# Branch B's output projection as two Strassen quads of seven products, with a new list schedule

## The chip, the cores and the metric

The kernel runs on one core of one Trainium2 chip. The metric is the device time of one execution in microseconds. The program holds one layer (512 positions, model width 1024, feed-forward width 2816), all in 32-bit floats.

## The reference

```python
def _mixer(x, mem, ...):
    h = _rmsnorm(x, norm_mix_g)
    p_a, p_b, q, p_g = jnp.split(h @ w_in, IN_SPLITS, axis=-1)
    gb, gc, v = jnp.split(p_a, 3, axis=-1)
    y_a = (gb * _causal_dwconv(gc * v, conv_a_w)) @ w_a_out
    u, ug = jnp.split(p_b, 2, axis=-1)
    u = _causal_dwconv(u * jax.nn.sigmoid(ug), conv_b_w) + conv_b_bias      # 31 taps
    y_b = jax.nn.silu(_layernorm(u, ln_b_g, ln_b_b)) @ w_b_out
    ...                                    # cross-attention into 256 memory tokens: o
    y_c = o @ w_att_out
    g = jax.nn.sigmoid((p_g + b_gate).reshape(bsz, seq, 3, D_MODEL))
    return (g[:, :, 0] * y_a + g[:, :, 1] * y_b + g[:, :, 2] * y_c) @ w_o

def reference(x, mem, ...):
    x = x + _mixer(x, mem, ...)
    h = _rmsnorm(x, norm_ffn_g)
    gt, up = jnp.split(_causal_dwconv(h @ w_up, conv_ffn_w), 2, axis=-1)
    return _rmsnorm(x + (jax.nn.silu(gt) * up) @ w_down, norm_final_g)
```

The change is in `y_b = ... @ w_b_out`, a product of 512 by 1024 by 1024.

## The kernel before

**Arithmetic.** Each 32-bit operand is split into a high part (a cast on ScalarE, the profile's ACT) and a low part (the rest, a subtraction on VectorE, DVE), and a product is three products of parts: high by high, low by high, high by low. Weights come in blocks of 512 KB (128 partitions by 1024). `split_job` turns a loaded block `wf` into `whi` (L494, ACT) and `wlo` (L498, DVE). In some places ACT writes the negated high part instead and an accumulating transfer, issued by GpSimd (POOL), adds the block once more, so that DVE is spared (`lo_from`, L515).

**Quads.** Most projections use Strassen's scheme in Winograd's form: two by two blocks of weights times two by two blocks of the activation in seven products instead of eight, f = 1 to 7 (`multiply`, L674). One such product is 24 matmuls of 256 columns here. Its operands are the blocks of the activation b00, b10, b11 and the sums t4 to t7, each with a high and a low part; `quad_loads` brings the weights and forms their sums in place (jobs s5, s6, s7, s3, by accumulating transfers where `by_dma` is set); `quad_reads` takes the results out of the banks of PSUM and adds them (r1 to r7). The three output projections of the branches were not quads: `merge_product` (L1406) runs eight plain units (four column groups m by two halves g), each 24 matmuls of 512 columns (L1416 to L1418), on `ybh`, `ybl` in branch B (br = 1). DVE multiplies the results by the gates (job weigh, L1449), and sums them over the branches into `mg` (L1467), whose four quarters are the operands of the last projection `w_o`. That one is a hand-written scheme of seven products a, b, f, c, d, e, g on `mgh` and `mgl`; the weights of a, b and d (`whoh`, `whol`) are split early and held in tiles that the quads' forms used before.

**Order.** TensorE's (PE) order is written out in `seq`, and hooks after certain products put the merge and other work in. All other instructions are jobs of the list scheduler `Jobs`: it runs when the program is built, gives each job a due time from the product that needs it, shifts it by the table `LATER`, holds back the kinds of job named in `AHEAD` until so long before their due time, and writes the instructions into each engine's queue in the order that comes out. So a change of a table, of a cost or of a job can move work of any engine in the whole program. Weights come in through six buffers `wf` and rings of tiles; four pairs of `whi` and `wlo` exist (`UNIT_BUFS`). SP issues plain loads, POOL accumulating ones; each issues in order.

**Stages.** In order of time: memory keys and values, the mixer's input projection with convolutions and attention between, the branches' output projections, `w_o` and the residual `x`, then `w_up` in quads with convolution and gate, `w_down`, the final norm and the output.

Of the kernel before, what the change touches and what calls it, by code (L numbers as in the profile page):

```python
# [8 lines left out]
F32 = mybir.dt.float32  # L9
F32R = mybir.dt.float32r  # L10
AF = mybir.ActivationFunctionType
ALU = mybir.AluOpType
# [49 lines left out]
PACE = 0.3  # L62
SEEN = {"PE": 0.2, "ACT": 0.14, "DVE": 0.12}
# [7 lines left out]
    "ACT high": -44, "ACT r1 glu": -9, "ACT r4 gate": 44, "ACT r4 up": -3, "ACT r5 glu": -7,  # L71
    "ACT sigmoid": 12, "ACT tap 1": 3, "ACT tp 3": -111, "ACT vh": 40, "ACT wh mix 5": 8,
# [9 lines left out]
    "ACT fh h2 t4": 5, "ACT high": 10, "ACT r5 glu": 10, "ACT r5 up": 5, "ACT sigmoid": 20,  # L82
    "ACT tap 1": 150, "ACT vh": 5, "ACT wh pd a": 5, "DVE rd g": 5, "DVE tot1": 10,
    "POOL s5 q": 10, "POOL wadd e": 5, "POOL xa": 40, "SP ld e 0": 20,
# [246 lines left out]
def hybrid_block_kernel(  # L331
# [139 lines left out]
    def split_job(unit, key, n_k, n, after, wide=None, lo_from=None, held=None):  # L471
# [62 lines left out]
    def block(w, col, k):  # L534

        return w[col // 256, k]
# [89 lines left out]
    def quad_loads(q, w, col0, col1, by_dma=False, take=("wf",), after=()):  # L626
# [9 lines left out]
        split_job((q, 1), u, 4, 256, [("ld", u)])  # L636
        split_job((q, 2), v, 4, 256, [("ld", v)])
# [22 lines left out]
        split_job((q, 4), r, 4, 256, [("ld", r)])  # L660
# [32 lines left out]
    def quad_reads(q, first, second, ring, after=()):  # L693
# [13 lines left out]
        def add(t, b):  # L707
# [13 lines left out]
            [(q, 3), ("r6", q)], use=[bank("b"), first])  # L721
        job(("r4", q), "ACT", actv(512), lambda: nc.scalar.activation(
# [327 lines left out]
    for h in range(HEADS):  # L1050
# [18 lines left out]
        for tp in range(2):  # L1069
# [23 lines left out]
            job(("exp", h, tp), "ACT", 0.84, exps,  # L1093
# [107 lines left out]
    for p in range(4):  # L1201
        job(("sg", p), "ACT", actv(1024), lambda p=p: nc.scalar.activation(
# [154 lines left out]
    for p in range(4):  # L1357
        split_pair(("acc", p), ("ybh", p), ("ybl", p), [("swish", p)])
# [25 lines left out]
    for p in range(4):  # L1384
# [13 lines left out]
    PARTS = {0: ("yah", "yal"), 1: ("ybh", "ybl"), 2: ("oh", "ol")}  # L1398
    PARTS_READY = {
        0: [("low", ("ya", p)) for p in range(4)],  # L1400
        1: [("low", ("acc", p)) for p in range(4)],
        2: [("ol", h, d) for h in range(HEADS) for d in range(2)],
    }
    W_OUT = {0: w_a_out, 1: w_b_out, 2: w_att_out}
# [26 lines left out]
    for br in (2, 0, 1):  # L1431
        for m in range(4):
            for g in range(2):
                unit_job(("merge", br, m, g), block(W_OUT[br], m * 256, g), lo_by_dma=br != 1 and 2 < 2 * m + g < 6)
# [9 lines left out]
            job(("sigmoid", br, m), "ACT", 2 * scaled_act(512), sigmoid,  # L1444
                ready_of(("gate", br, m // 2), m % 2) + [("ldp",)], use=[gate])
            for j in range(2):
# [12 lines left out]
            elif br == 1:  # L1459
                for r in range(2):  # L1460
                    part = ("mg", r, m // 2)

                    def merged(m=m, gate=gate, r=r, part=part):
# [9 lines left out]
                        weighed + [("sum", 0, m)] + ([("sum", 1, m - 1, r)] if m % 2 else []),  # L1473
# [5 lines left out]
    late_rows = [("merge", 1, 0, 1)]  # L1479
# [28 lines left out]
    }  # L1508

# [8 lines left out]
    for i in range(2):  # L1518
# [17 lines left out]
        for p, key, after in (  # L1536
# [5 lines left out]
            split_job(("wo", p, i), ("wo", key, i), 2, 512, [after], held=WO_HELD.get((p, i)))  # L1542
# [194 lines left out]
    for q in range(QUADS):  # L1737
# [12 lines left out]
        job(("silu", q), "ACT", actv(1024), lambda q=q: nc.scalar.activation(  # L1750
# [18 lines left out]
    for do in (  # L1769
# [41 lines left out]
        (GATE[1, 1], 3): lambda: [pe_merge(1, m) for m in range(4)],  # L1811
# [55 lines left out]
    first = [(UP[0], 1), (UP[0], 2), "tr2", (UP[1], 1), "tr3", (UP[1], 2), (UP[2], 1), (UP[0], 5), (UP[2], 2), (UP[0], 6), (UP[1], 5), (UP[0], 7), (UP[0], 3), (UP[0], 4), (UP[1], 6), (UP[2], 5), (UP[1], 7), (UP[2], 6), (UP[1], 4), (UP[1], 3)]  # L1867
# [254 lines left out]

    for p in DOWN:
# [13 lines left out]
    for t in range(NT):  # L2137
# [7 lines left out]
        else:  # L2145
# [11 lines left out]
        job(("sv", t), "DVE", 0.75, lambda t=t: left_scaled(t),  # L2157
            [("rc", t)] + ([("rd", "end", 1)] if t == 2 else []))
# [65 lines left out]
```

## Time and profile before

| what | value |
|---|---|
| time, median of 3 runs | 926.52 us (926.11 to 926.7) |
| profiled execution | 926.69 us, of which the span of the trace is 924.7 us |
| granted TensorE clock | 0.999 |
| busy: PE, DVE, ACT, POOL | 916.1, 838.7, 669.0, 127.0 us |
| moved by DMA | 190.60 MB |

The span runs from the first to the last instruction; 2.0 us of the profiled execution lie outside it. The engines run side by side, so their busy times overlap; an engine's idle time matters only where another waits for it.

### The profile page before, as it was taken

The page shows a single profiled execution, that of the slowest core. Times are in us where ns is not written, and L with a number is a line of the kernel's source. Part 1 is how long each engine was busy: PE and PEld are TensorE (multiplying, and loading weights), DVE is VectorE, ACT ScalarE, POOL GpSimd, SP SyncE. Part 2 cuts the span into 40 slices and gives each one's busy share as a digit, 9 for nine tenths or more (in the row PEclk, how much of TensorE's full clock was granted, in tenths as well). Part 3 has the DMA queues.
Part 4 walks back from the last instruction along what each step waited for, and adds up shares of the span by engine and source line. Part 5 has one row for each costly group of instructions (what it writes and reads, how often), then busy time and mean ns, then how long its engine had stood idle before and what let it go on. Part 6 is the DMA issues. An engine that isn't in the chain of part 4 may idle for free.

```text
span 924.7 us, 16795 instructions
## 1 busy us (share of the span) xinstructions
PE 916.1 (99%) x6677; PEld 861.9 (93%) x6677; DVE 838.7 (91%) x952; ACT 669.0 (72%) x911; POOL 127.0 (14%) x153
## 2 busy tenths in 40 slices
PE   9999999999999999999999999999999999999997
PEld 8999999999989999999899888899999999988886
DVE  6997999979989999999986788898989889999987
ACT  7567988859889877778855763767676676765566
POOL 0111121100111211110100001021211121002120
PEclk9999999999999999999999999999999999999999
DMA  9999877956678789887855598499999996789962
GB/s 353 369 297 225 177 133 142 233 134 114 180 190 223 159 189 226 187 197 202 198 119 168 164 318 181 117 219 302 283 222 233 218 182 120 201 269 319 260 131 91
DMA packets 54222, 190.60 MB, mean 206 GB/s; under 512 B 6144, under 2 KB 6272, under 8 KB 54144
## 3 DMA queue, kind: packets, MB, share of 16 engines
q0 software_dynamic: 20880, 75.24, 46.0%
q1 hardware_dynamic: 32976, 114.02, 34.3%
q8 instruction: 52, 0.85, 0.4%
q10 hardware_dynamic: 288, 0.27, 0.1%
q14 instruction: 26, 0.21, 0.1%
HBM read 185.31 MB, written 4.19 MB: 205 GB/s over the span
## 4 chain that ended last, share of the span: by engine, by line
PE 94%; DMA 3%; ACT 1%; DVE 0%; SPq 0%; issue 0%; POOLq 0%; DVEq 0%; ACTq 0%
PE bank L674 57%; PE bank L446 7%; PE bank L447 7%; PE bank L445 7%; PE bank L1416 5%; PE bank L1418 5%; PE bank L1417 5%; DMA wf<-in_w_up 2%; PE bank L928 2%; DMA wf<-in_w_v 1%; ACT whi L494 1%; PE ss L801 0%; PE bank L1165 0%; PE bank L1653 0%; DVE wlo L498 0%
## 5 line engine op out<-in xcount | busy, mean ns | idle before, releaser
L494 ACT CAST whi<-wf 128x1024 fp32r<-128x1024 f32 (+1 forms) x190 | 197.4, 1042 | 91.7 <-PE bank L674 47.1
L498 DVE TENSOR_TENSOR wlo<-wf,whi 128x1024 fp32r<-128x1024 f32 (+1 forms) x184 | 222.0, 1211 | 28.5 <-ACT whi L494 27.9
L1237 ACT ACTIVATE tp<-u,pk 128x510 f32<-128x510 f32 (+22 forms) x184 | 119.4, 705 | 5.1 <-DVE acc L1244 4.8
L1244 DVE TENSOR_TENSOR acc<-acc,tp 128x1020 f32<-128x1020 f32 (+22 forms) x92 | 109.2, 1188 | 5.8 <-ACT tp L1237 3.8
L632 POOL DMA_DIRECT2D wf<-in_w_in x45 | 39.0, 873 | 236.3 <-DVE wlo L498 175.4
L674 PE MATMUL bank<-ft6h,whi 128*128 128x256 f32 x232 | 64.4, 277 | 0.7 <-ACT gt L701 0.7
L674 PE MATMUL bank<-ft5l,whi 128*128 128x256 f32 x232 | 64.4, 278 | 0.0
L674 PE MATMUL bank<-fb10h,whi 128*128 128x256 f32 x232 | 64.4, 277 | 0.0
L674 PE MATMUL bank<-ft6h,wlo 128*128 128x256 f32 x232 | 64.3, 277 | 0.0
L674 PE MATMUL bank<-ft5h,wlo 128*128 128x256 f32 x232 | 64.3, 277 | 0.0
L674 PE MATMUL bank<-fb00h,whi 128*128 128x256 f32 x232 | 64.3, 277 | 0.0
L674 PE MATMUL bank<-ft7h,whi 128*128 128x256 f32 x232 | 64.3, 277 | 0.0
L674 PE MATMUL bank<-ft7l,whi 128*128 128x256 f32 x232 | 64.3, 277 | 0.0
L674 PE MATMUL bank<-ft7h,wlo 128*128 128x256 f32 x232 | 64.3, 277 | 0.0
L674 PE MATMUL bank<-fb11h,whi 128*128 128x256 f32 x232 | 64.3, 277 | 0.0
L674 PE MATMUL bank<-ft5h,whi 128*128 128x256 f32 x232 | 64.3, 277 | 0.0
L674 PE MATMUL bank<-ft6l,whi 128*128 128x256 f32 x232 | 64.3, 277 | 0.0
L674 PE MATMUL bank<-fb00l,whi 128*128 128x256 f32 x232 | 64.2, 277 | 0.0
L674 PE MATMUL bank<-fb00h,wlo 128*128 128x256 f32 x232 | 64.2, 277 | 0.0
L674 PE MATMUL bank<-fb10h,wlo 128*128 128x256 f32 x232 | 64.1, 276 | 0.0
L674 PE MATMUL bank<-fb10l,whi 128*128 128x256 f32 x232 | 64.1, 276 | 0.0
L674 PE MATMUL bank<-fb11l,whi 128*128 128x256 f32 x232 | 64.1, 276 | 0.0
(401 smaller groups left out, 3170.5 us busy)
## 6 DMA issues: line engine op xcount, KB each, us to landing
wf<-in_w_in SPq DMA_DIRECT2D x50, 512.0 KB, 5.0
wf<-in_w_in POOLq DMA_DIRECT2D x45, 512.0 KB, 5.9
wf<-in_w_up POOLq DMA_DIRECT2D x30, 512.0 KB, 7.6
wf<-in_w_up SPq DMA_DIRECT2D x29, 512.0 KB, 6.3
wf<-in_w_down SPq DMA_DIRECT2D x15, 512.0 KB, 4.6
wf<-in_w_att_out SPq DMA_DIRECT2D x8, 512.0 KB, 3.7
wf<-in_w_a_out SPq DMA_DIRECT2D x8, 512.0 KB, 4.2
wf<-in_w_b_out SPq DMA_DIRECT2D x8, 512.0 KB, 4.3
```

Of the source, the lines that this page charges most:

```text
L445: nc.tensor.matmul(ps, s_hi, w_hi, start=start, stop=False, skip_group_check=again)
L446: nc.tensor.matmul(ps, s_hi, w_lo, start=False, stop=False, skip_group_check=again)
L447: nc.tensor.matmul(ps, s_lo, w_hi, start=False, stop=stop, skip_group_check=again)
L494: nc.scalar.copy(parts[0], src())
L498: nc.vector.tensor_tensor(lo, src(), hi.bitcast(F32), op=ALU.subtract)
L632: nc.gpsimd.dma_start(out=tiles[key], in_=block(w, col[c], k), accum_op=ALU.add)
L674: nc.tensor.matmul(ps[:, c, :], w[:, k, at], a[k], start=first and n == 0, stop=i == 3 and n == 2, skip_group_check=again,)
L1237: nc.scalar.activation(two(("tp", p, s))[:, j, s:], two(("u", p))[:, j, : SEQ - s], AF.Copy, scale=weight(j),)
L1244: nc.vector.tensor_tensor(a, a, two(("tp", p, s))[:, :, s:], op=ALU.add)
L1416: nc.tensor.matmul(ps, w_hi[:, i, at], hi, start=first, stop=False)
L1417: nc.tensor.matmul(ps, w_hi[:, i, at], lo, start=False, stop=False)
L1418: nc.tensor.matmul(ps, w_lo[:, i, at], hi, start=False, stop=last)
```

## The change

Branch B's eight plain units become two quads, ("mq", 0) and ("mq", 1), run product by product in the order f = 1, 5, 2, 6, 7, 4, 3, the two in turn. The activation after its norm is formed as the seven operands, in halves: b00, b10, b11 are blocks of `acc`, t5, t7, t6, t4 are half sums on DVE, t7, t6 and t4 in place. The weights' sums s5, s6, s7, s3 are accumulating transfers. The results are read as in other quads, but the last one is weighed by the gate straight from its bank. The lows of `w_o`'s held weights for a and b now come by accumulating transfer (`WO_LOWS`) instead of from DVE, and the held tiles come free after the last quad's products. The rows of `x` for the residual are loaded after a product of the second quad. The scheduler's costs count 1.28 us for a load of ACT's function table at four jobs (`TABLE`); both tables are new, and the `w_up` stage starts with another order of products. The last output tile's left half is scaled and sent in two halves.

```diff
+TABLE = 1.28
...
 LATER = {
-    "ACT high": -44, "ACT r1 glu": -9, "ACT r4 gate": 44, "ACT r4 up": -3, "ACT r5 glu": -7,
...
+    "DVE h2 t4": -36, "DVE kl": -6, "DVE kt": 11, "DVE mgl a": 32, "DVE mgl f": 25,
...
 AHEAD = {
-    "ACT fh h2 t4": 5, "ACT high": 10, "ACT r5 glu": 10, "ACT r5 up": 5, "ACT sigmoid": 20,
+    "ACT kh": 40, "ACT r1 up": 80, "ACT r5 gate": 20, "ACT r5 up": 40, "ACT sg": 80,
...
             if held:
                 last = next(f for f in OPERAND if OPERAND[f] == held)
-                before = [(QUAD_ORDER[-1], last)]
+                before = [(("mq", 1), last)]
...
+        low = lambda f, c, k: block(w, col[c], k) if f in lows else None
+        split_job((q, 1), u, 4, 256, [("ld", u)], lo_from=low(1, 0, 0))
...
-    for p in range(4):
-        split_pair(("acc", p), ("ybh", p), ("ybl", p), [("swish", p)])
...
+    for e in range(2):
+        top, end = ("acc", e), ("acc", 2 + e)
+        done = lambda *ps: [("swish", p) for p in ps]
+        b00 = y_parts("b00", e, lambda e=e: rows_of(e, 0), done(e), [top])
+        b10 = y_parts("b10", e, lambda e=e: rows_of(2 + e, 0), done(2 + e), [end])
+        y_parts("b11", e, lambda e=e: rows_of(2 + e, 1), done(2 + e), [end])
...
+        job(("y", "t7", e), "DVE", dve(512), lambda e=e: nc.vector.tensor_tensor(
+            rows_of(e, 1), rows_of(2 + e, 1), rows_of(e, 1), op=ALU.subtract),
+            [Y5 + (e,)] + done(2 + e), use=[top, end])
...
-            for g in range(2):
-                unit_job(("merge", br, m, g), block(W_OUT[br], m * 256, g), lo_by_dma=br != 1 and 2 < 2 * m + g < 6)
+            for g in range(2) if br != 1 else ():
+                unit_job(("merge", br, m, g), block(W_OUT[br], m * 256, g),
+                         lo_by_dma=2 < 2 * m + g < 6)
...
+                quad = ("mq", m // 2)
+                if m % 2 == 0:
+                    quad_loads(quad, w_b_out, m * 256, m * 256 + 256, by_dma=True, lows=MQ_LOWS)
+                    quad_reads(quad, ("y", m), ("y", m + 1), ANY, all_but_4=True)
...
+                    def weigh_last(m=m, gate=gate, at=at, quad=quad):
+                        t = two(gate)[:, :, at]
+                        nc.vector.scalar_tensor_tensor(
+                            t, halves(("bank", quad, "a")), -1.0, t, op0=ALU.mult, op1=ALU.mult)
...
-    late_rows = [("merge", 1, 0, 1)]
+    late_rows = [(("mq", 1), 1)]
...
+    WO_LOWS = [(p, i) for p in "ab" for i in range(2)]
...
-        (GATE[1, 1], 3): lambda: [pe_merge(1, m) for m in range(4)],
+        (GATE[1, 1], 3): lambda: [
+            multiply_job(("mq", q), f, "y") for f in (1, 5, 2, 6, 7, 4, 3) for q in range(2)],
...
-    first = [(UP[0], 1), ..., (UP[2], 1), (UP[0], 5), (UP[2], 2), (UP[0], 6), (UP[1], 5), (UP[0], 7), ...]
+    first = [(UP[0], 1), ..., (UP[2], 1), (UP[0], 5), (UP[1], 5), (UP[0], 6), (UP[2], 2), (UP[0], 7), ...]
...
+        if t < last:
+            job(("sv", t), "DVE", 0.75, lambda t=t: left_scaled(t),
+                [("rc", t)] + ([("rd", "end", 1)] if t == 2 else []))
+        else:
+            for i in range(2):
+                job(("sv", t, i), "DVE", 0.4, lambda i=i: last_scaled(i), [("rc", t)])
```

The order moves at three places that the prediction speaks of. The first is DVE between the last sum of the merge and the third product of `w_o`, f. `mg` are the merged quarters, `mgl` the low parts of operands of `w_o`'s products, `bank` results. Before, f's sum is the first of the two 1024-wide rows on `mg_796_6183` and its low part `mgl_850_6468`:

```order
L1467 TENSOR_TENSOR mg_835_6393<-g_338_2496,g_746_5812 128x512
L1467 TENSOR_TENSOR mg_839_6400<-g_338_2496,g_746_5812 128x512
L1550 TENSOR_TENSOR mg_796_6183<-mg_839_6400,mg_796_6183 128x1024
L1572 TENSOR_TENSOR mgl_841_6408<-mg_835_6393,mgh_840_6406 128x512
L451 SCALAR_TENSOR_TENSOR mg_795_6181<-mg_796_6183,mg_795_6181 128x1024
L1572 TENSOR_TENSOR mgl_850_6468<-mg_796_6183,mgh_846_6449 128x1024
```

After, on the same engine, from the read of the second quad's last product (bank_794_6194) on; f's sum is `mg_845_6613` and its low part `mgl_865_6694`, c's are `mg_828_6480` and `mgl_864_6692`:

```order
L715 TENSOR_TENSOR y_790_6185<-y_790_6185,bank_794_6194 128x2x256
L1562 TENSOR_TENSOR mg_845_6613<-g_293_2183,g_716_5565 128x512
L1542 TENSOR_TENSOR g_742_5780<-y_790_6185,g_742_5780 128x2x256
L1562 TENSOR_TENSOR mg_845_6613<-g_312_2339,g_717_5568 128x512
L1562 TENSOR_TENSOR mg_847_6632<-g_352_2597,g_742_5780 128x512
L1562 TENSOR_TENSOR mg_847_6632<-g_354_2613,g_746_5814 128x512
L1650 TENSOR_TENSOR mg_845_6613<-mg_847_6632,mg_845_6613 128x1024
L504 TENSOR_TENSOR wlo_849_6636<-wo_789_6181,whi_848_6635 128x1024
L504 TENSOR_TENSOR whol_851_6641<-wo_829_6482,whoh_850_6640 128x1024
L457 SCALAR_TENSOR_TENSOR mg_828_6480<-mg_845_6613,mg_828_6480 128x1024
L504 TENSOR_TENSOR wlo_857_6663<-wo_797_6225,whi_856_6662 128x1024
L504 TENSOR_TENSOR whol_860_6669<-wo_837_6524,whoh_859_6668 128x1024
```

Behind these stand the low parts of c and of f, in that order, then four additions into `x`, two weight sums, one more addition, and c's first weight split:

```order
L1672 TENSOR_TENSOR mgl_864_6692<-mg_828_6480,mgh_862_6674 128x1024
L1672 TENSOR_TENSOR mgl_865_6694<-mg_845_6613,mgh_855_6659 128x1024
L1727 TENSOR_TENSOR x1_842_6590<-x1_842_6590,bank_843_6598 128x512
L1727 TENSOR_TENSOR x1_846_6616<-x1_846_6616,bank_844_6602 128x512
L1727 TENSOR_TENSOR x1_842_6590<-x1_842_6590,bank_852_6643 128x512
L1727 TENSOR_TENSOR x1_846_6616<-x1_846_6616,bank_853_6647 128x512
L800 TENSOR_TENSOR wo_829_6482<-wo_829_6482,wo_789_6181 128x1024
L800 TENSOR_TENSOR wo_837_6524<-wo_837_6524,wo_797_6225 128x1024
L1727 TENSOR_TENSOR x1_861_6672<-x1_861_6672,bank_866_6697 128x512
L504 TENSOR_TENSOR wlo_870_6726<-wo_829_6482,whi_869_6725 128x1024
```

So between the last sum and f's low part there stood one 1024-wide instruction and a half-wide one; now there are six 1024-wide ones.

The second place is SP's queue from the first rows of `x` (`x1`) on. Before, where three loads of `w_up` stand among them, and three more were issued earlier still:

```order
L1484 DMA x1_819_6307<-in_x 128x1024
L1484 DMA x1_822_6314<-in_x 128x1024
L524 DMA wf_825_6323<-in_w_up 128x1024
L1484 DMA x1_828_6329<-in_x 128x1024
L524 DMA wf_833_6362<-in_w_up 128x1024
L524 DMA wf_834_6366<-in_w_up 128x1024
L1484 DMA x1_838_6398<-in_x 128x1024
```

After, where these are the first loads of `w_up` in the program:

```order
L1580 DMA x1_861_6672<-in_x 128x1024
L1580 DMA x1_863_6689<-in_x 128x1024
L1586 DMA gffn_867_6705<-in_norm_ffn_g 128x1024
L530 DMA wf_873_6738<-in_w_up 128x1024
L530 DMA wf_874_6749<-in_w_up 128x1024
L530 DMA wf_879_6780<-in_w_up 128x1024
```

All six loads of `w_up` that came before the gain of the second norm (`gffn`) now stand behind it.

The third place is DVE behind the scaling of the normalised branch B (`acc` by `rows`, four rows that read the same in both). Before:

```order
L498 TENSOR_TENSOR wlo_765_5957<-wf_736_5739,whi_764_5956 128x1024
L1349 TENSOR_TENSOR ybl_768_6020<-acc_170_1091,ybh_766_5991 128x1024
L1349 TENSOR_TENSOR ybl_770_6026<-acc_352_2604,ybh_767_5994 128x1024
L1349 TENSOR_TENSOR ybl_773_6058<-acc_444_3269,ybh_771_6054 128x1024
L1349 TENSOR_TENSOR ybl_778_6089<-acc_553_4208,ybh_772_6056 128x1024
```

After, where the operands b00 and t5 come in halves between weight splits:

```order
L504 TENSOR_TENSOR wlo_765_5965<-wf_747_5843,whi_764_5964 128x1024
L1391 TENSOR_TENSOR fb00l_767_6000<-acc_174_1146,fb00h_766_5999 128x512
L1412 TENSOR_TENSOR y_768_6032<-acc_174_1146 128x512
L1391 TENSOR_TENSOR fb00l_767_6000<-acc_314_2344,fb00h_766_5999 128x512
L1412 TENSOR_TENSOR y_768_6032<-acc_314_2344 128x512
L504 TENSOR_TENSOR wlo_770_6035<-wf_754_5891,whi_769_6034 128x1024
L504 TENSOR_TENSOR wlo_774_6067<-wf_741_5777,whi_773_6066 128x1024
```

From there to the low part of t6 (`ft6l`), the operand of the seventh product, there are 8 instructions of 1024 columns and 21 of 512. Over the whole program DVE's rows grow from 905 to 930, ACT's from 734 to 761, POOL's from 151 to 162, as consecutive equal rows count as one.

More of the change, by code (lines that the diff above doesn't have):

```diff
@@ L624, in form_jobs, with quad_loads @@
             parts(key, lambda at=at: four(at), [(act, key)], [at])
[L626 removed]
+    def quad_loads(q, w, col0, col1, by_dma=False, take=("wf",), after=(), lows=()):
         col = (col0, col1)
@@ L691, in hybrid_block_kernel, with quad_reads @@
     form_ready = {}
-    def quad_reads(q, first, second, ring, after=()):
+    def quad_reads(q, first, second, ring, after=(), all_but_4=False):
         f, s = lambda: two(first), lambda: two(second)
@@ L1355, in split_pair, with rows_of, y_parts, pieces @@
             use=[src, hi])
-    for p in range(4):
-        split_pair(("acc", p), ("ybh", p), ("ybl", p), [("swish", p)])
+    def rows_of(p, r):
+        return two(("acc", p))[:, :, r * HALF : (r + 1) * HALF]
+    def y_parts(key, e, src, after, use):
+        last = next(f for f in OPERAND if OPERAND[f] == key)
+        def pieces(views):
+            if len(views) == 1:
+                return [(slice(0, 2), views[0][:, 2 * e : 2 * e + 2, :])]
+            if e == 0:
+                return [(slice(0, 2), views[0][:, :2, :])]
+            return [(slice(0, 1), views[0][:, 2:3, :]), (slice(1, 2), views[1].unsqueeze(1))]
+        def high():
+            if e == 0:
+                form_tile("y", key)
+            for at, h in pieces(form["y", key, "views"][0]):
+                nc.scalar.copy(h, src()[:, at, :])
+        def low():
+            hi, lo = form["y", key, "views"]
+            for (at, h), (_, l) in zip(pieces(hi), pieces(lo)):
+                nc.vector.tensor_tensor(l, src()[:, at, :], h.bitcast(F32), op=ALU.subtract)
+        hk, lk = ("fh", "y", key, e), ("fl", "y", key, e)
+        job(hk, "ACT", actv(512), high,
+            after + [(("gate", 1, 1), last)] + ([("fh", "y", key, 0)] if e else []), use=use)
+        job(lk, "DVE", dve(512), low, [hk], use=use)
+        form_ready.setdefault(("y", key), []).append(lk)
+        return lk
```

77 lines of the change are left out of this document (58 added, 19 removed), and 16 rows, old and new, of tables (AHEAD, LATER).

## The prediction

> **What bounds the kernel now.** I read the page first, then the waits of TensorE, then windows, then the order of time on single engines. In the page, the engines' busy time, the DMA queues, and the chain by engine:
>
> ```profile
> span 924.7 us, 16795 instructions
> PE 916.1 (99%) x6677; PEld 861.9 (93%) x6677; DVE 838.7 (91%) x952; ACT 669.0 (72%) x911; POOL 127.0 (14%) x153
> ...
> q0 software_dynamic: 20880, 75.24, 46.0%
> q1 hardware_dynamic: 32976, 114.02, 34.3%
> ...
> PE 94%; DMA 3%; ACT 1%; DVE 0%; SPq 0%; issue 0%; POOLq 0%; DVEq 0%; ACTq 0%
> ```
>
> PE is busy for 99% of the span and carries 94% of the chain. What it ever waited for (us in total, times, longest):
>
> ```profile
> PE bank L1764 <- POOL ident masks.py:199: 1.4, 1, 1.4
> PE bank L674 <- ACT gt L701: 0.7, 1, 0.7
> PE bank L928 <- DVE wlo L876: 0.2, 1, 0.2
> PE bank L446 <- DVE wlo L498: 0.2, 1, 0.2
> ```
>
> So time goes down only with PE's work, and whatever makes an operand late adds to it. How much room the others have, by windows (busy PE, PEld, DVE, ACT, POOL; then granted clock, DMA share, GB/s):
>
> ```profile
> 300.00:400.00 100.00, 100.00 (x883) 100.00 (x882) 99.47 (x107) 78.35 (x108) 17.75 (x21) 1.00 0.85 193
> 490.00:515.00 25.00, 25.00 (x173) 23.07 (x172) 15.51 (x17) 16.69 (x21) 0.00 (x0) 1.00 0.45 135
> 515.00:561.00 46.00, 46.00 (x205) 38.05 (x204) 37.82 (x43) 27.33 (x33) 3.49 (x4) 1.00 0.80 254
> 561.00:580.00 19.00, 19.00 (x85) 15.46 (x84) 16.35 (x19) 7.35 (x8) 2.62 (x3) 1.00 0.84 186
> 580.00:600.00 20.00, 20.00 (x101) 16.61 (x100) 17.19 (x23) 13.97 (x22) 1.73 (x2) 1.00 0.38 109
> 600.00:650.00 50.00, 49.31 (x423) 48.91 (x423) 43.46 (x49) 35.96 (x50) 8.68 (x10) 1.00 0.99 259
> ```
>
> Between 490 and 600 us, the stage that is changed, DVE has 9.5 + 8.2 + 2.7 + 2.8 = 23.1 us to spare, and DMA 13.8 + 9.2 + 3.0 + 12.4 = 38.4 us. From 600 on DMA is full.
>
> **The change part by part.** *The products.* PE in order of time: the last product of 24 by 256 columns, the first matmul of branch B, the first of w_o, the first of w_o's third product f, and f's third matmul.
>
> ```profile
> 512.31 0.28 PE L674 MATMUL bank<-fb11h,whi 128*128 128x256 f32 x1
> 515.03 0.39 PE L1416 MATMUL bank<-ybh,whi 128*128 128x512 f32 x1
> 558.57 0.39 PE L445 MATMUL bank<-whoh,mgh 128*128 128x512 f32 x1
> 569.76 0.39 PE L445 MATMUL bank<-whi,mgh 128*128 128x512 f32 x1
> 570.23 0.39 PE L447 MATMUL bank<-whi,mgl 128*128 128x512 f32 x1
> ```
>
> The eight plain units took 558.57 - 515.03 = 43.54 us. One quad product takes 515.03 - 512.31 = 2.72 us, and fourteen take 38.1. I take 38.3, as a product whose columns come in more pieces (t4) is a little longer. Gain: 5.2 us.
>
> The step is 43.54 us / 192 = 227 ns for 512 columns, and 2.72 / 24 = 113 ns for 256, so twice half a matmul costs the same as one and the gain is near one eighth. The Trainium skill (TensorE: Matmul & The Clock Gate, "Wait — 56ns, not 53.3ns?") gives a warm matmul N / 2.4 GHz plus a fixed 2.5 ns, so halving the columns would cost that fixed part twice: 192 x 215.8 - 336 x 109.2 ns = 4.7 us of gain, and a time 0.5 us above mine. The trace's steps are longer at both sizes; the rows decide.
>
> *What the other engines get.* DVE, in order of time: the start of the normalised branch B, the weight split behind it, the first read after the plain units, then the merge's last sums, f's sum (L1550) and f's low part (565.02).
>
> ```profile
> 504.39 4.60 DVE L1328 TENSOR_TENSOR acc<-acc,rows 128x1024 f32<-128x1024 f32 x4
> 508.92 1.22 DVE L498 TENSOR_TENSOR wlo<-wf,whi 128x1024 fp32r<-128x1024 f32 x1
> 558.77 0.69 DVE L1449 TENSOR_TENSOR g<-bank,g 128x512 f32<-128x512 f32 x1 [1.50 <-PE bank L1418]
> 560.82 1.29 DVE L1467 TENSOR_TENSOR mg<-g,g 128x512 f32<-128x512 f32 x2
> 562.14 1.23 DVE L1550 TENSOR_TENSOR mg<-mg,mg 128x1024 f32<-128x1024 f32 x1
> 563.28 0.68 DVE L1572 TENSOR_TENSOR mgl<-mg,mgh 128x512 fp32r<-128x512 f32 x1
> 563.89 1.22 DVE L451 SCALAR_TENSOR_TENSOR mg<-mg,mg 128x1024 f32<-128x1024 f32 x1
> 565.02 1.22 DVE L1572 TENSOR_TENSOR mgl<-mg,mgh 128x1024 fp32r<-128x1024 f32 x1
> 566.16 0.68 DVE L1627 TENSOR_TENSOR x<-x,bank 128x512 f32<-128x512 f32 x1
> 566.76 1.22 DVE L1572 TENSOR_TENSOR mgl<-mg,mgh 128x1024 fp32r<-128x1024 f32 x1
> ```
>
> From start to start a 1024-wide instruction takes 1.14 us (565.02 to 566.16) and a 512-wide one 0.60. DVE gains 6 weight splits and loses 4 held lows (+2.3); 14 half lows replace 4 whole ones (+3.8); 8 half sums (+4.8) and 6 half reads (+3.6) are new: 14.5 us against 23.1 - 5.2 = 17.9 to spare. ACT gains about as much and has 44.7 us idle there: no cost. DVE's total fits; what counts is where its waits for PE leave it too late.
>
> *Start of the quads.* From 508.92, where DVE stands as before, to t6's low part there are 8 instructions of 1.14 and 21 of 0.60: 21.7 us, so 530.6, and up to 1.2 more for ACT's highs. Product seven wants it at 515.03 + 6 x 2.72 = 531.4. Between 0 and 0.4 late; I take 0.2. The operands before it come 2 to 6 us early by the same count.
>
> *Into w_o.* Call E the end of the last quad product. DVE's read of its bank starts 0.2 us behind it (558.57 to 558.77). Then, by the order, come six halves (3.6), the sum 1.14, two weight splits 2.28, c's sum 1.14, two splits 2.28, c's low part 1.14 and f's low part 1.22: f is ready at E + 13.0. PE wants it behind products a and b and two matmuls, 570.23 - 558.57 = 11.66 us after E. Before, it was ready at 566.24, 4.0 us ahead; now it is 1.3 us late. Then c: from E + 12.9, four halves, two sums, a half and a split end at E + 19.4. PE wants it at E + 11.19 + 5.6 + 0.23 + 1.3 = E + 18.3 at the latest rate of f, so 1.1 more. Together 2.4 us. These lines start from E, so they hold if DVE is free by then. If the 11 rows ahead of that read run late, up to 0.7 is added, as much as one half row and its wait; I take 0.3. d, e and g have a slack of 0.6 to 3 us by the same count.
>
> *Transfers.* By the queues' rows, one accumulating block takes 0.46 x 924.7 / 75.24 x 0.524 MB = 3.0 us of the DMA engines, a plain one 1.5. Twelve more accumulates (8 in the quads, 4 for w_o) make 35.5 us, in the 38.4 that are free. The six early loads of w_up go behind the load of the norm's gain:
>
> ```profile
> 547.53 3.79 SPq L524 DMA_DIRECT2D wf<-in_w_up  x2
> ...
> 569.96 0.33 SPq L1490 DMA_DIRECT2D gffn<-in_norm_ffn_g  x1
> ```
>
> Behind it, 6 x 1.5 + 3.0 = 12 us of w_up meet 12.4 us that were free from 580 to 600. I take nothing for it; the second rival has the other end.
>
> *The end.* The last tile's scaling in two halves:
>
> ```profile
> 918.64 0.42 DVE L2082 TENSOR_TENSOR x<-x,bank 128x256 f32<-128x256 f32 x1 [1.09 <-PE bank L447]
> 920.16 0.75 DVE L2118 SCALAR_TENSOR_TENSOR x<-x,cols,gfin 128x512 f32<-128x512 f32 x1
> 920.16 0.72 ACT L2112 ACTIVATE x<-x,cols 128x512 f32<-128x512 f32 x1 [0.23 <-DVE cols L2153]
> 920.91 0.38 ACTq L2114 DMA_DIRECT2D out<-x  x1
> ```
>
> A half takes about 0.42 instead of 0.75, but ACT's half of the tile is sent at 920.91 as before: between 0.3 gained and 0.1 lost by one more transfer; I take 0.1 gained. *The counted table loads*, the moved rows of x and the order of the first w_up products change when things are issued, not how much; with the new tables they move rows in the whole mixer, where DVE has 0.53 us idle in 100. I take nothing, with 0 to 3 us lost as bounds (third rival).
>
> Sum: -5.2 + 0.2 + 2.4 + 0.3 - 0.1 = -2.4. Against the profiled execution 926.69 that is 924.3; the median of the runs shown lies 0.17 below it. Forecast 924.1, and 923.0 to 925.3 with the bounds of these terms. What can be told from no change here is about 0.2%, 1.85 us: 924.67 and 928.37 are the limits.
>
> **The rivals.** *First: the products' gain arrives nearly whole.* For it: DVE has the room in sum, and PE never waited in this stage. Against it: f's low part is behind six wide rows that cannot start before E. It needs ACT or the transfers to change nothing and the steps on DVE to be shorter than 1.14. Time 926.5 - 5.3 = 921.2, up to 923.
>
> *Second: transfers become the bound, and it is slower.* The place is the start of the w_up stage. The stage of w_o now needs 35.5 us of the 38.4 - 2.6 = 35.8 that are free by the time w_up starts, 2.6 us earlier. No reserve is left: each us of DMA time that stays idle early, where the weights wait for a buffer, is a us of w_up blocks that are not there when PE wants them, and from 600 on DMA is at 0.99 and can't make it up. For it: 0.55 of 490 to 515 was idle, and a load waits for buffers that PE sets free. Against it: not all six blocks are wanted at once, and before the change the ring was full at 580. With 6 us left idle the time is 924.1 + 6 = 930; it decides for slower from 4.3 us on. The Trainium skill (DMA: Bandwidth & Descriptors, "Issuing engines are not separate DMA queues") says that transfers of all issuing engines run on the same 16 DMA engines and interleave. By that rule the accumulates of POOL are paid out of SP's loads, which speaks for this rival; the trace agrees as far as the two queues together make up the 0.99.
>
> *Third: the new tables cost as much as is left.* In the mixer DVE has no idle time to catch up with, so a split put behind another 1.14 us row reaches PE once its lead is used. Two or three such places give back 2.4 us: 926.5, between 925 and 929. Against it: before, PE waited nowhere in the mixer, and DVE's work there is the same.
>
> **How the numbers follow.** Forecast 0.44, of which 0.33 are below 924.67. First rival 0.24, all faster. Second 0.17, all slower. Third 0.15: 0.10 the same, 0.05 slower. Faster 0.33 + 0.24 = 0.57, the same 0.11 + 0.10 = 0.21, slower 0.17 + 0.05 = 0.22. The forecast's own range is 923.0 to 925.3; the range goes down to the first rival and up to 929.5, which leaves out the worse half of the second.
>
> **What would show it.** After: quads of 38.3 us between the first matmul on y and w_o; PE waits for `mgl` at f (1.3 to 2) and for `wlo` at c (about 1), and none of 0.5 elsewhere between 515 and 600; the first w_up product near 596.5. I am wrong by the first rival if those two waits are missing, by the second if PE waits for whi or wlo between 597 and 650 by more than 2 us, with ACT waiting for DMA; by the third if waits show before 500.

## The result: 929.92 us, 0.36% slower, and the profile after

The changed kernel took 929.92 us (median of 6 executions, 928.39 to 930.6), the kernel before 926.65 us on the same chip (926.11 to 926.8). The ratio is 1.0036, interval 1.0026 to 1.0046: slower by 3.3 us, where 2.4 us of gain had been forecast. The time lies just above the range's upper end, 929.5. The profiled execution took 929.3 us, its span 927.5 us, 2.8 us more than before.

From the page of the changed kernel, the span, the engines' busy time, the two queues and the chain:

```profile
span 927.5 us, 17130 instructions
PE 914.6 (99%) x6821; PEld 866.5 (93%) x6821; DVE 852.0 (92%) x980; ACT 685.2 (74%) x938; POOL 137.1 (15%) x165
...
q0 software_dynamic: 22608, 81.54, 48.9%
q1 hardware_dynamic: 33120, 114.02, 34.1%
...
PE 91%; DVE 5%; DMA 3%; issue 1%; ACT 0%; SPq 0%; DVEq 0%; POOL 0%; POOLq 0%; ACTq 0%
```

PE is busy for 1.5 us less than before, although part of its work ran at half clock (below), and the kernel is longer: PE waits. What it waited for (us in total, times, longest):

```profile
PE bank L681 <- ACT gt L708: 2.4, 1, 2.4
PE bank L452 <- DMA whol<-in_w_o: 2.2, 2, 1.5
PE bank L1864 <- POOL ident masks.py:199: 1.4, 1, 1.4
PE bank L681 <- DVE wlo L504: 0.5, 1, 0.5
PE bank L452 <- DVE wlo L504: 0.4, 1, 0.4
```

The wait for `ident` stands in both kernels; the others are new or larger. The windows of the stages (busy PE, PEld, DVE, ACT, POOL; clock, DMA share, GB/s) show the room that is left:

```profile
300.00:400.00 100.00, 100.00 (x883) 100.00 (x882) 93.63 (x99) 74.45 (x100) 17.94 (x21) 1.00 0.84 189
...
515.00:561.00 46.00, 45.30 (x365) 43.23 (x365) 45.05 (x63) 37.53 (x51) 8.69 (x10) 1.00 1.01 264
561.00:580.00 19.00, 17.03 (x74) 13.31 (x73) 18.97 (x21) 7.81 (x9) 4.34 (x5) 1.00 1.05 335
580.00:600.00 20.00, 20.00 (x108) 17.05 (x107) 19.74 (x25) 16.73 (x25) 2.59 (x3) 1.00 0.89 221
600.00:650.00 50.00, 47.33 (x403) 46.83 (x401) 40.48 (x45) 33.00 (x46) 8.69 (x10) 1.00 1.00 261
```

Between 515 and 580 us DVE has 0.98 us left and the DMA engines none. Before, DVE had 10.8 us there.

Where the time went is read from the start of the same matmul in both kernels. Two such rows of PE before, the first w_up product and the first product of the fourth quad of w_up, (up 3, 5):

```profile
599.01 0.28 PE L674 MATMUL bank<-fb00h,whi 128*128 128x256 f32 x1
...
652.12 0.28 PE L674 MATMUL bank<-ft5h,whi 128*128 128x256 f32 x1
```

PE after: the quads' start, the first of w_o, four rows at which PE stopped in w_o and the start of f between them, the first w_up product, the stop ahead of (up 2, 6), and (up 3, 5):

```profile
514.81 0.28 PE L681 MATMUL bank<-fb00h,whi 128*128 128x256 f32 x1
553.17 0.39 PE L451 MATMUL bank<-whoh,mgh 128*128 128x512 f32 x1
...
556.37 0.50 PE L452 MATMUL bank<-whol,mgh 128*128 128x512 f32 x1
...
560.13 0.50 PE L452 MATMUL bank<-whol,mgh 128*128 128x512 f32 x1 [0.69 <-DMA whol<-in_w_o]
...
564.73 0.51 PE L452 MATMUL bank<-whol,mgh 128*128 128x512 f32 x1 [1.53 <-DMA whol<-in_w_o]
...
567.40 0.39 PE L451 MATMUL bank<-whi,mgh 128*128 128x512 f32 x1
...
573.70 0.50 PE L452 MATMUL bank<-wlo,mgh 128*128 128x512 f32 x1 [0.43 <-DVE wlo L504]
...
597.34 0.28 PE L681 MATMUL bank<-fb00h,whi 128*128 128x256 f32 x1
...
650.25 0.38 PE L681 MATMUL bank<-ft6h,whi 128*128 128x256 f32 x1 [2.40 <-ACT gt L708]
...
654.40 0.41 PE L681 MATMUL bank<-ft5h,whi 128*128 128x256 f32 x1
```

| place | before | after | difference |
|---|---|---|---|
| start of the quads | 515.03 | 514.81 | -0.22 |
| first of w_o | 558.57 | 553.17 | -5.40 |
| f of w_o | 569.76 | 567.40 | -2.36 |
| first w_up product | 599.01 | 597.34 | -1.67 |
| (up 3, 5) | 652.12 | 654.40 | +2.28 |
| end of the span | 924.7 | 927.5 | +2.8 |

So the quads bring their 5.2 us; w_o gives back 3.73 us, and the first third of w_up another 4.3, most of it at one place, ahead of (up 2, 6). There ACT is the releaser. POOL's sums (from issue on) and ACT's rows after:

```profile
634.04 0.86 POOL L638 DMA_DIRECT2D ('up', 3)_966_7341<-in_w_up  x1 [10.42 <-ACT uu L731]
634.58 1.22 POOL L638 DMA_DIRECT2D wf<-in_w_up  x1
```

```profile
644.41 1.05 ACT L500 CAST whi<-('up', 3)_966_7341 128x1024 fp32r<-128x1024 f32 x1 [5.12 <-DMA ('up', 3)_966_7341<-in_w_up]
645.48 1.28 ACT L1850 ACT_TABLE_LOAD   x1
646.77 1.06 ACT L1850 ACTIVATE gtc<-gtc 128x1024 f32<-128x1024 f32 x1
648.18 1.05 ACT L500 CAST whi<-wf 128x1024 fp32r<-128x1024 f32 x1 [0.35 <-DMA wf<-in_w_up]
649.13 0.59 ACT L731 ACTIVATE uu<-bank 128x512 f32<-128x512 f32 x1
649.62 0.58 ACT L708 COPY gt<-bank 128x512 f32<-128x512 f32 x1
```

ACT stands for 5.12 us in front of the block of (up 3), whose sum s5 took from 634.04 to 644.4. Behind it, in order, wait the table load, the silu, the weights of (up 2, 6) and the read of its bank, for which PE waits. Yet PE wants (up 3, 5) a whole product later than (up 2, 6). But the cast of (up 2, 6) at 648.18 waits once more, 0.35 us for its own block: that is the second sum on POOL, s6 of (up 2), sent 0.54 us behind the first, and by the DMA view it landed 13.5 us after its issue, against 10.3 for the first. So without ACT's stop of 5.12 us alone the cast could have come at most 0.35 earlier. Before, two sums on POOL, the second of them that of (up 3), and the casts on ACT:

```profile
634.29 0.86 POOL L632 DMA_DIRECT2D wf<-in_w_up  x1 [2.19 <-DVE wlo L498]
637.36 0.86 POOL L632 DMA_DIRECT2D ('up', 3)_949_7143<-in_w_up  x1 [2.21 <-DMA ('up', 3)_949_7143<-in_w_up]
```

```profile
644.56 2.00 ACT L494 CAST whi<-wf 128x1024 fp32r<-128x1024 f32 x2 [1.04 <-DMA wf<-in_w_up]
...
648.34 1.05 ACT L494 CAST whi<-('up', 3)_949_7143 128x1024 fp32r<-128x1024 f32 x1 [0.92 <-DMA ('up', 3)_949_7143<-in_w_up]
```

Before, the sum took as long (637.36 to 648.3) and was sent 3.3 us later, 3.07 us behind the sum ahead of it instead of 0.54 ahead of another. Its cast stood last in line, and ACT's stop of 0.92 us cost PE nothing.

Behind PE's wait comes a second loss. Windows of 1 us after it, with the granted clock third from the right:

```profile
651.00:652.00 1.00, 1.00 (x10) 1.00 (x9) 1.00 (x3) 1.00 (x3) 0.64 (x1) 0.87 1.05 283
652.00:653.00 1.00, 1.00 (x7) 1.00 (x6) 1.00 (x2) 1.00 (x3) 0.00 (x0) 0.50 1.11 274
653.00:654.00 1.00, 1.00 (x7) 1.00 (x7) 1.00 (x2) 0.81 (x2) 0.00 (x0) 0.50 1.12 250
654.00:655.00 1.00, 1.00 (x6) 1.00 (x6) 0.96 (x2) 0.36 (x1) 0.76 (x2) 0.50 1.04 229
655.00:656.00 1.00, 1.00 (x10) 1.00 (x9) 1.00 (x2) 1.00 (x2) 1.00 (x2) 0.93 1.07 229
```

For 3.4 us TensorE runs at half clock, which costs 0.13 + 3 x 0.50 + 0.07 = 1.70 us.

### The profile page after: what moved, and what is told of

It reads as the page before. It is cut to its first block, busy times and chain, and to the rows that moved or that the text cites. A ratio compares the mean times of both kernels' runs of the same rounds, so it can differ in the third digit from the quotient of the medians.

```text
span 927.5 us, 17130 instructions
## 1 busy us (share of the span) xinstructions
PE 914.6 (99%) x6821; PEld 866.5 (93%) x6821; DVE 852.0 (92%) x980; ACT 685.2 (74%) x938; POOL 137.1 (15%) x165
## 4 chain that ended last, share of the span: by engine, by line
PE 91%; DVE 5%; DMA 3%; issue 1%; ACT 0%; SPq 0%; DVEq 0%; POOL 0%; POOLq 0%; ACTq 0%
PE bank L681 60%; PE bank L453 6%; PE bank L452 6%; PE bank L451 6%; PE bank L1486 3%; PE bank L1488 3%; PE bank L1487 3%; PE bank L937 2%; DMA ('up', 3)_966_7341<-in_w_up 2%; DVE wlo L504 1%; DMA y_sum<-in_w_down 1%; DVE mg L1562 1%; DVE mgl L1672 1%; PE bank L1864 0%; PE ss L810 0%
## 5 line engine op out<-in xcount | busy, mean ns | idle before, releaser
L500 ACT CAST whi<-wf 128x1024 fp32r<-128x1024 f32 x206 | 214.8, 1044 | 102.0 <-PE bank L681 53.5
L504 DVE TENSOR_TENSOR wlo<-wf,whi 128x1024 fp32r<-128x1024 f32 (+1 forms) x200 | 241.6, 1212 | 31.4 <-ACT whi L500 28.4
L1246 ACT ACTIVATE tp<-u,pk 128x482 f32<-128x482 f32 (+22 forms) x184 | 118.9, 704 | 4.2 <-DVE acc L1253 3.7
L1253 DVE TENSOR_TENSOR acc<-acc,tp 128x1022 f32<-128x1022 f32 (+22 forms) x92 | 109.2, 1188 | 4.0 <-ACT tp L1246 2.7
L638 POOL DMA_DIRECT2D wf<-in_w_in x50 | 44.2, 891 | 231.8 <-DVE wlo L504 185.7
L681 PE MATMUL bank<-ft6h,whi 128*128 128x256 f32 x248 | 69.4, 280 | 2.4 <-ACT gt L708 2.4
L681 PE MATMUL bank<-ft6h,wlo 128*128 128x256 f32 x248 | 69.4, 280 | 0.0
L681 PE MATMUL bank<-ft6l,whi 128*128 128x256 f32 x248 | 69.4, 280 | 0.0
L681 PE MATMUL bank<-fb11h,wlo 128*128 128x256 f32 x248 | 68.6, 277 | 0.5 <-DVE wlo L504 0.5
L681 PE MATMUL bank<-ft5h,whi 128*128 128x256 f32 x248 | 68.9, 278 | 0.0
```

Source lines behind the costliest of these rows:

```text
L500: nc.scalar.copy(parts[0], src())
L504: nc.vector.tensor_tensor(lo, src(), hi.bitcast(F32), op=ALU.subtract)
L638: nc.gpsimd.dma_start(out=tiles[key], in_=block(w, col[c], k), accum_op=ALU.add)
L681: nc.tensor.matmul(ps[:, c, :], w[:, k, at], a[k], start=first and n == 0, stop=i == 3 and n == 2, skip_group_check=again,)
L1246: nc.scalar.activation(two(("tp", p, s))[:, j, s:], two(("u", p))[:, j, : SEQ - s], AF.Copy, scale=weight(j),)
L1253: nc.vector.tensor_tensor(a, a, two(("tp", p, s))[:, :, s:], op=ALU.add)
```

## The experiments

The expectations weigh theories by letter. Theory A is the second rival: transfers bound the whole stretch, and too many of them ahead of w_up leave a backlog that w_up pays. Theory B: two places are late on their own; DVE is late in w_o in any case, and near 650 us ACT's queue stands in front of the sum for (up 3, 5). From experiment 5 on, theory C: the loss near 650 is the order of two transfers, the sums for (up 2, 6) and (up 3, 5); theory D: w_up is bound by transfers altogether, and the wait only moves. In "light" kernels an accumulating transfer or a DVE row touches a part of its columns only and leaves out the rest.

**1. The twelve added transfers made light.**

```diff
-                    out=parts[1], in_=lo_from, accum_op=ALU.add), ...
+                    out=parts[1][:, :n_low], in_=lo_from[:, :n_low], accum_op=ALU.add), ...   # n_low = 128 for w_o
...
+            n = 128 if q[0] == "mq" else 1024
```

> The changed kernel, in which the twelve accumulating transfers that the change adds move 128 of 1024 columns (the rest of these weight sums is left out); every engine's order is the same. Theory A, transfers bound the whole stretch: the two waits for whol (2.2 us) go, the backlog at the start of w_up goes, and with it the waits of 0.5 and 2.4 us near 645 to 650 and the half clock behind them (1.7): 929.9 - 6.8 = 923.1. Theory B, DVE comes late to w_o in any case and the loss at 650 is made locally, by one block of w_up and ACT's queue: f's low part is ready at 567.25 in the changed kernel and f starts at 567.4, so only about 0.6 us come back, and the waits at 645 to 650 stay: 929.3.

Measured: 928.51 us, ratio 1.0030 (1.0020 to 1.0041). What PE waited for:

```profile
PE bank L453 <- DVE mgl L1675: 2.3, 1, 2.3
PE bank L684 <- ACT gt L711: 2.3, 1, 2.3
```

The DMA share falls from 1.01 to 0.71 in 515 to 561 and from 0.89 to 0.74 in 580 to 600, and there is idle DMA time again (only 561 to 580 stays full, at 1.01), but the wait near 650 is as long as before: a backlog left by the added transfers is not its cause, and theory A falls; the time is near theory B's 929.3. The Trainium skill (DMA: Bandwidth & Descriptors, "Issuing engines are not separate DMA queues") has the transfers of all issuing engines on the same 16 DMA engines, as the prediction said beside that rival; the trace agrees, as the two queues' shares between 600 and 650 us in the changed kernel, 58.5% and 41.6%, make up the whole. In w_o the waits for `whol` are gone, and f's low part takes their place: DVE's row for it stands where it stood (564.88 against 564.90).

**2. The held lows of w_o back on DVE.**

```diff
-    WO_LOWS = [(p, i) for p in "ab" for i in range(2)]
+    WO_LOWS = []
```

> The changed kernel without the four accumulating transfers for w_o's weights of a and b: DVE makes these lows again (4 instructions of 1.14 us), and the list schedule then puts five loads of w_up ahead of the norm's gain. Theory A: the waits for whol go and w_up is ready earlier, 926 or less. Theory B: DVE, already late behind the last quad product, becomes later by up to 4.6 us at f, and the loss at 650 stays if the same cast stands in ACT's queue: 930 to 933.

Measured: 941.33 us, ratio 1.0163 (1.0150 to 1.0176). This is above both expectations, as the list schedule came out otherwise as a whole: PE waits 11.3 us at f for ACT's `mgh`, and the wait of 2.4 for `gt` stays. It says little of the lows, but a lot of how far one edit moves this schedule.

**3. The old order of the first w_up products.** `first` as before, with (UP[2], 2) and (UP[2], 6) ahead of where they now stand, everything else as changed.

> The changed kernel with the order of the first w_up products as before the change. Theory A: the backlog of transfers is the same, so PE waits about 3 us between 620 and 655 wherever the products stand: 929 to 930. Theory B: in this order ACT's function table and the first silu come before the cast that waited 5.1 us for its block, so the 2.4 us wait and the half clock go: about 926.

Measured: 934.89 us, ratio 1.0083 (1.0071 to 1.0095), outside both expectations. PE waits 3.0 us for `gt` and 3.0 for `ft5l`. So the order of the products alone is not what broke the place; with the new tables the old order is worse.

**4. The cast of (up 3, 5) held back on ACT.**

```diff
+        ahead["wh", (("up", 3), 5)] = 3.0
```

> The changed kernel with one job held back in the schedule: ACT's cast of the block (up 3, product 5), which stood ahead of the table load, the silu and the read that PE waited for, and itself waited 5.1 us for its transfer. Now the table load and the silu stand ahead of it. Theory A: PE waits instead for that block's parts, 929 to 930. Theory B: of the 2.4 us at most 0.5 stay, and the half clock behind it (1.7) goes: 926 to 926.5.

Measured: 931.12 us, ratio 1.0053 (1.0039 to 1.0067). The cast now stands behind that of (up 2, 6), but ACT then waits 2.02 us for this one's own block, which lands at 648.2 as in the changed kernel: the sum of (up 3) had been sent first and shares the engines:

```profile
648.22 1.04 ACT L501 CAST whi<-wf 128x1024 fp32r<-128x1024 f32 x1 [2.02 <-DMA wf<-in_w_up]
```

The wait for `gt` is 2.8 us. Neither theory had this time, and B's reading of the place near 650 falls: with ACT free of the stop, the block of (up 2, 6) is still not there.

**5. The sum of (up 2, 6) sent first.**

```diff
+        ahead["s5", ("up", 3)] = 5.0
```

> The changed kernel with one accumulating transfer held back, so that on POOL the sum for product (up 2, 6), which PE wants first, stands ahead of the sum for (up 3, 5); ACT and DVE follow in a few rows there. In the changed kernel the first of these landed at 648.2, 13.6 us after its issue, the other at 644.3. Theory C, the loss near 650 is the order of these two transfers: the sum lands near 645, PE waits under 0.5 us there, and without the half clock behind the wait the time is 925.5 to 926.5. Theory D, w_up is bound by transfers altogether: another block is as late, PE waits 2 us or more within 20 us of it, 929 to 931.

Measured: 929.1 us, ratio 1.0027 (1.0017 to 1.0038). Now ACT stands 5.38 us in front of (up 2, 6), and the low part of another product's weights, which waits in DVE's line behind that, stops PE for 2.7 us. That is what theory D expected. Whichever sum comes first lands 10 us after it was sent, the second 13 (10.0 and 13.2 us here, 10.3 and 13.5 in the changed kernel), and rows that others need stand behind their casts.

**6. Both sums light, and 7. only that of (up 3, 5).** Number 7 is number 6 with one of the two sums whole again.

```diff
+            n = 128 if (q, c, k) in ((('up', 3), 1, 1), (('up', 2), 0, 0)) and key[1] == 's' else 1024
...
+            n = 128 if (q, c, k) == (('up', 3), 1, 1) and key[1] == 's' else 1024
```

> The changed kernel, every order the same, in which just these two accumulating transfers move 128 of 1024 columns (the rest of these two weight sums is left out). Theory C: both land within 5 us, the waits of 0.5 and 2.4 us near 645 to 650 go, 925.5. Theory D: the next blocks of w_up are late instead, 928 to 930.

> Only the accumulating transfer for s5 of (up, 3) carries 128 of its 1024 columns, so those weights are left partly unsummed; s6 of (up, 2) is whole. If the cast of s5's block, which stands ahead on ACT, is all that is late: 926.9 to 927.5, with no wait over 1 us near 650. If s6 of (up, 2) is late by itself: the wait for whi or gt stays at 1.5 to 2.5 us, 928.5 to 930.

Measured: 926.85 us (ratio 1.0000, 0.9992 to 1.0009) and 926.94 us (1.0006, 0.9998 to 1.0015). The second one's waits of PE in w_up, and ACT's casts of the two blocks:

```profile
PE bank L683 <- DVE wlo L504: 0.5, 1, 0.5
PE bank L683 <- ACT gt L710: 0.3, 1, 0.3
```

```profile
643.31 1.05 ACT L500 CAST whi<-('up', 3)_966_7341 128x1024 fp32r<-128x1024 f32 x1 [2.91 <-PE bank L683]
...
647.14 1.06 ACT L500 CAST whi<-wf 128x1024 fp32r<-128x1024 f32 x1 [0.40 <-DMA wf<-in_w_up]
```

ACT no longer stands before this block for DMA, and one 0.5 MB transfer cut to an eighth at this place is worth 929.92 - 926.94 = 3.0 us: the wait, and the half clock behind it (no window from 648 to 657 is below 1.00). From the first w_up product to (up 3, 5) it takes 53.11 us before, 57.06 in the changed kernel, 53.63 with this sum light and 52.70 with both. The other sum, whole in number 7, now lands 11.4 us after its issue instead of 13.5, and is still what the cast of (up 2, 6) waits for last (0.40 us). Theory D's 928 to 930 for number 6 did not come, and number 7 lies in the 926.9 to 927.5 of its first case. This names the w_up place: the two sums sent 0.54 us apart. How much of it is the DMA time that the first takes from the second, and how much the rows that stand behind the casts, is not separated; with experiment 4, ACT's line alone is not enough.

**8. That of the two that can be had in earnest: s6 of (up 2) as an addition on DVE.**

```diff
-        quad_loads(up, w_up, q * 256, D_FF + q * 256, by_dma=True,
+        quad_loads(up, w_up, q * 256, D_FF + q * 256, by_dma=q not in (2,),
```

> The whole computation; only the weights' sum s6 of (up, 2) is a DVE addition instead of an accumulating transfer (its s7 waits for it), which moves the list schedule of the w_up stage behind it. w_o is as in the changed kernel. If the two sums are late because two accumulating transfers stand in line at a DMA share of 1.0, one fewer lets the other, s5 of (up, 3), land some 3 us earlier: the wait near 650 is gone or under 1 us, and the time is 926.8 to 928. If the wait only moves to the next sum in the line, or DVE pays with 1.1 us for the addition, 929 to 931.

Measured: 930.93 us, ratio 1.0049 (1.0032 to 1.0066). The other sum lands hardly earlier (9.9 us from issue to cast), with another transfer sent 0.8 us behind it, and on DVE another product's low part, wanted at once, stands behind its split:

```profile
PE bank L681 <- DVE wlo L504: 3.5, 1, 3.5
```

```profile
646.14 1.23 DVE L504 TENSOR_TENSOR wlo<-('up', 3)_966_7340,whi 128x1024 fp32r<-128x1024 f32 x1 [0.62 <-ACT whi L500]
...
647.94 1.22 DVE L504 TENSOR_TENSOR wlo<-wf,whi 128x1024 fp32r<-128x1024 f32 x1
```

**9. f's low part earlier, with the twelve transfers light; 10. the same with the sums swapped, transfers whole.**

```diff
-    ... "DVE mgl f": 25,
+    ... "DVE mgl f": -30,
```

> The changed kernel with the twelve added accumulating transfers at 128 of 1024 columns as before, and with DVE's low part of w_o's third operand f moved ahead of four 1024-wide instructions (4.5 us). If both, the transfers of whol and DVE's order, bind w_o, the waits for whol (2.2) and for mgl (2.3 with light transfers alone) are both gone, and the first product of w_up starts near 595 instead of 597.3. If what follows is bound by transfers of w_up, the gain is lost again by 660 and the time is 928 to 929; if not, it is 925.5 to 927.

> The changed kernel with whole transfers, f's low part moved ahead as in the run before, and the two accumulating transfers of w_up swapped. The waits for whol stay (2.2), so f gains under 0.8 us over the swap alone: 925 to 926 by theory C, 929 to 930 by theory D.

Measured: 929.78 us (1.0035, 1.0023 to 1.0048) and 929.96 us (1.0040, 1.0025 to 1.0056). The wait at f is gone in number 9, and c pays: 1.5 us for its `whi`, 1.2 for its `wlo`; the first w_up product starts at 600.40, where about 595 was expected. Number 10, near theory D's time, has 1.9 us for `whol`, 1.4 at c and 2.4 in w_up. DVE has no room in w_o, so an order that serves f takes it from c.

**11. The twelve transfers light and DVE relieved in w_o** (the sums of operands and weights at 128 of 1024 columns, the additions into x at 64 of 512).

```diff
-            row = two(("x1", 2 * r + t))[:, h, :]
+            row = two(("x1", 2 * r + t))[:, h, :64]
...
+            tiles[out][:, :128], tiles[x][:, :128], tiles[y][:, :128]), after,
```

> The changed kernel, every order the same, with the twelve added accumulating transfers at 128 of 1024 columns, and with DVE's in-place work behind the last quad product cut too: the sums for f, c, d and e and the two weight sums to 128 of 1024 columns, the additions into x to 64 of 512 (the rest of these sums is left out). If w_o is bound by both, transfers of whol and DVE's queue, neither wait of PE is left between 553 and 590: f's low part comes 2.3 us earlier than 567.2, c's split 5.8 earlier than 572.4, and w_up starts 3 to 4 us earlier than 597.3. The loss near 650 then comes as before, since it follows PE's progress and not the clock on the wall: 926 to 927. If instead w_up's transfers are a backlog, the time stays at 928.5 to 930.

Measured: 925.27 us, ratio 0.9985 (0.9976 to 0.9994), 3.2 us below the light transfers alone and lower than both expectations. w_o now loses 1.1 us: from 5.03 ahead of before at its start to 3.95 in the first quad of w_up (-5.40 to -1.38 in the changed kernel). The wait of 2.3 for `gt` stays. DVE relieved with the transfers whole was not run.

**12. All three: number 11 with the two w_up sums of number 6.**

> As the run before, and the two late sums of w_up at 128 of 1024 columns as in the earlier run with those two alone (which gave 3 us). If the two places, w_o and the two sums, hold the whole loss, the gain of the products arrives: 926.4 - 5.2 = 921.2, up to 922.5 with what is left of small waits. If a third place is as tight, 924 or more.

Measured: 922.82 us, ratio 0.9956 (0.9942 to 0.9970), between the two expectations. PE's rows at the first of w_o and at (up 3, 5), to be held against 558.57 and 652.12 before:

```profile
552.98 0.39 PE L451 MATMUL bank<-whoh,mgh 128*128 128x512 f32 x1
...
648.91 0.28 PE L684 MATMUL bank<-ft5h,whi 128*128 128x256 f32 x1
```

With both places relieved, 3.2 of the 5.6 us ahead arrive. It is no version to use, since it leaves work out, some of which the kernel before had to do too. It shows that the two places together hold up to the 7.1 us between 929.92 and 922.82: w_o 4.6 (929.92 to 925.27), w_up 2.5 more.

## Why the prediction was wrong

**The products: right.** 38.3 us were forecast from matmul to matmul; 553.17 - 514.81 = 38.36 us. The gain is 43.54 - 38.36 = 5.18, against 5.2. The first rival, that this gain arrives nearly whole, falls by what comes after.

**Start of the quads: right in effect.** 0.2 of loss was taken for t6. PE lists no wait between the quads' start and w_o, but the first two steps of t6's product take 0.42 us (531.13 to 531.55) where two steps take 0.23: the 0.2 came, and lies in the 38.36. The 0.22 by which the quads start earlier lie ahead of them.

**Into w_o: the place right, the size and the releaser wrong.** 2.4 + 0.3 us were forecast, 3.73 were lost. From start to start the stops cost more than their listed wait: 556.37 0.28 (not listed), 560.13 0.96, 564.73 1.81, 573.70 0.70, in sum 3.75, about 0.28 more for each stop than PE's list has. Of it 3.05 belong to the lows of a's and b's weights that come by transfer. The prediction had costed these four transfers in us of free DMA time, but not by when each must land; that term was missing. On DVE, the read of the last quad product's bank, f's low part behind c's, and c's split:

```profile
554.35 0.68 DVE L715 TENSOR_TENSOR y<-y,bank 128x512 f32<-128x512 f32 x1
...
564.90 2.35 DVE L1672 TENSOR_TENSOR mgl<-mg,mgh 128x1024 fp32r<-128x1024 f32 x2
...
572.43 2.35 DVE L504 TENSOR_TENSOR wlo<-wo,whi 128x1024 fp32r<-128x1024 f32 x2
```

f's low part ends at 567.25, E + 14.1 where E + 13.0 was counted: the count of rows was right, but DVE began it at E + 1.2 instead of E + 0.2, so 1.0 us late, not 0.3. With the transfers out of the way (experiment 1) this stops PE at f for 2.3 us, against 1.3 to 1.6 in the sum. In the changed kernel the transfers' stops come first and hide it; at c, 0.43 is listed for the 1.1 forecast. So the two causes stand side by side: taking the transfers away brings 1.4 us (experiment 1), both 4.6 (experiment 11).

**Transfers at w_up: this is the step that turned the sign.** "I take nothing for it" stands for 4.3 us (from 1.67 ahead to 2.66 behind at 657.50). From the first quad of w_up, 1.38 ahead (614.61 to 613.23), to (up 3, 5), 2.28 behind: the stops at 645.06 (0.8) and 650.25 (2.7) and 1.3 of half clock, less 1.0 for before's own stop for `gt`, make 3.8, against 3.66 measured. The second rival had the place and the direction, and its sign in the profile is there in part: PE stopped for over 2 us with ACT waiting for DMA, though for `gt` and not for `whi` or `wlo`. Its mechanism is not: with the early transfers light the stop stays. That its 930 was met is luck, as 1.0 us of the excess was lost in w_o. What the runs show in its place: two sums of w_up were sent 0.54 us apart into DMA engines that were full, the one that PE wanted first landed 13.5 us after its issue, and the read of `gt` stood behind its cast on ACT. With one or both of the two light the stretch is about as short as before (experiments 6 and 7); exchanging the sums moves the wait (experiment 5), exchanging their casts leaves it (experiment 4). The prediction had put "the order of the first w_up products" and the new tables under edits that "change when things are issued, not how much", and took nothing for them in the mixer, where indeed nothing was lost (no wait there; DVE even has 6 us in 100 to spare); w_up, with DMA at 0.99 before the change, was where it had to be looked for.

**The end: 0.1 of gain forecast, 0.1 of loss seen**, between the difference in w_down (2.66 at 821 us) and that of the span, 2.8.

By rows: -0.22 - 5.18 + 3.73 + 4.33 + 0.1 = +2.8, the difference of the spans. The median lies 0.6 above the profiled execution.

**What stays open.** Which part of the change sent the two sums together: the new tables, the order `first`, or the loads of w_up that now start behind the norm's gain. In experiment 3 putting `first` back alone did not help. Loads as early as before were not tried. Of the versions that compute everything none is below the kernel before.

## What to carry to other kernels

An added transfer has two prices: its time on the DMA engines, and the moment at which it must have landed; where the engines' share is near 1.0, allow the landing time that the neighbouring rows show (here 10 us for 0.5 MB, 13 where another was sent just ahead) and count back from the product that needs it. Then read the in-order engine behind that landing: what stands after the waiting row is late too, whether it depends on the transfer or not. And where two late operands stand side by side, an experiment that relieves one of them shows too little (1.4 us here, 4.6 for both); relieve both, and then each.

## What the hardware showed unexpectedly

A stop of TensorE can cost twice. After the 2.4 us of waiting at 650 in the changed kernel, the granted clock was 0.50 for 3.4 us, 1.70 us lost. The same 1.70 us followed the wait of 2.3 us at f in experiment 1 and the 3.5 us in experiment 8; the 11.3 us of experiment 2 were followed by 5.1 us lost, three times as much. It doesn't always come: not after the 2.3 us near 650 in experiment 1, and not after the stops of 0.7 and 1.5 us in w_o in the changed kernel, though two stops of 1.5 and 1.2 us close together, at c in experiment 9, had it. It doesn't explain the spread from 928.39 to 930.6 us within the changed kernel: 930.41 came with a mean clock of 0.999, 929.3 with 0.997. The Trainium skill (TensorE: Matmul & The Clock Gate, "What's actually happening") has a free-running window of 4096 cycles at 1.2 GHz, 3413 ns, and half rate after at least one idle window. The length of the stretch agrees; the condition doesn't, as waits of 2.2 to 2.4 us were enough here. Such a window would let a wait of the same length bring the slow stretch in one place and not in another; no run here tests that.
